# First attention block: scores as two fp32r matmuls over 128 partitions instead of one fp32 matmul over 64

## The chip, the cores and the metric

The kernel runs on one core of a Trainium2 chip. The core has five engines with a program each: TensorE (PE, with its weight loads shown apart as PEld), VectorE (DVE), ScalarE (ACT), GpSimd (POOL) and SyncE (SP), which here only issues DMAs. Each engine works through its own list in order and waits for others by semaphores. The metric is the time of one execution in microseconds (us) on the device; several runs are made and their median is given.

## The reference

Two transformer blocks over 512 tokens of width 1024, all in float32. What the change touches is the attention of the first block: 16 query heads of 64 dimensions share 2 key/value heads (8 query heads each), every token sees the 128 tokens up to itself, and each head has a sink logit in its softmax.

```
q, k, v, pz, ga, gp = jnp.split(xn @ w_in[l] + b_in[l], SPLITS, axis=-1)
sc = einsum('bhgqd,bkhd->bhgqk', q_block, k_two_blocks) / sqrt(64)   # 128 queries x 256 keys
sc = where(0 <= qpos - kpos < 128, sc, -1e30)
p  = softmax(concat([sc, sink]))[..., :-1]
y_a = (p @ v_two_blocks) @ w_attn_up
y_p = multiscale_pool(pz) @ w_pool_up
h = h + (sigmoid(ga) * y_a + sigmoid(gp) * y_p) @ w_o
```

Behind it stand, untouched, a mixture-of-experts layer (16 experts out of 16384 for each of 8 heads of a token) and a second block with dilated attention and a gated feed-forward.

## The kernel before, in words

Activations of the projections lie feature-major: 128 features on the partitions, 512 tokens in the free dimension. Each float32 matrix that is multiplied at full width is split into two fp32r parts, high (`whi`, `xh`) and low (`wlo`, `xl`), and a product is made of three fp32r matmuls (high-high, high-low, low-high: `mm3`, L137 to L140). One block of the input projection, 128 output features by 512 tokens, is 8 x 3 = 24 such matmuls (`zblock`, L234). The weights of a block come by a DMA on SP's queue into one of three raw buffers (`wload`, L127), ACT rounds them to the high part (L132) and DVE subtracts to get the low part (L134).

The input projection has 30 blocks: blocks 0 to 7 queries, 8 keys, 9 values, 10 to 13 the pooling branch, 14 to 29 the gates of the two branches. A query block holds two heads: head b of the first key/value group on partitions 0 to 63 and head b of the second on 64 to 127. DVE writes the queries with bias and the factor 1/8 to `qT` (L261); ACT writes keys and values with their bias (L263). `b_in`, `qT`, `kT` stay in SBUF.

Attention (L301 to L358) goes over 4 blocks of 128 queries (i) and 2 key/value groups (g). For each of 8 heads one fp32 matmul over the 64 partitions of the group makes 128 queries x 256 keys (128 keys for i = 0) of scores (L313); in the trace it shows as two records of the engine and two weight loads. Two heads share a PSUM tile `sc`, of which there are two. DVE adds the mask and takes the row maximum (L315), ACT takes the exponentials with their sum (L328), PE transposes the 128x128 pieces (L339), ACT and DVE by turns copy the transposes to SBUF (L342, L344), and PE multiplies them with the values (L348, fp32, two records each). DVE divides by the sums (L351), and the result is transposed and split for the next projection (L356).

The 16 gate blocks (L361 to L367) follow in the text, but no wait ties them to attention: the scheduler lays out each engine's list ahead of time by its own estimate of when things are ready, and puts matmuls of the gate blocks (`mm` in the rows) between those of attention. Their sigmoid is ACT's (L366). ACT holds one set of function tables at a time: between a sigmoid and an exponential it loads a table. The gates' results `sg` lie in the pool `sgp`, which stands until the block's end. After attention come `w_attn_up`, `w_pool_up`, the merge and `w_o`, and `hres`, the input for the residual, is loaded into the space that attention leaves (L370 to L372).

`gain` (L68) loads a row of 1024 gains into one of two buffers of the tag "gain": first g_mix, then g_ffn and ln_final_g, for the stages behind.

Of the kernel before, what the change touches and what calls it, by code (L numbers as in the profile page):

```python
# [8 lines left out]
F32 = mybir.dt.float32  # L9
F32R = mybir.dt.float32r  # L10
# [3 lines left out]
AF = mybir.ActivationFunctionType  # L14
OP = mybir.AluOpType
# [3 lines left out]
S = 512  # L19
# [24 lines left out]
def body(ctx: ExitStack, tc: tile.TileContext, A: dict, out: bass.AP):  # L44
    nc = tc.nc
    V, SC, PE, GP, SY = nc.vector, nc.scalar, nc.tensor, nc.gpsimd, nc.sync
# [19 lines left out]
    gn = ctx.enter_context(tc.tile_pool(name="gn", bufs=2, reuse_waits="tile"))  # L66
# [6 lines left out]
    def f(ap):  # L73
        return ap.bitcast(F32)
# [120 lines left out]
    with ExitStack() as st:  # L195
# [3 lines left out]
        sgp = st.enter_context(tc.tile_pool(name="sgp", bufs=1, reuse_waits="tile"))  # L199
# [42 lines left out]
        with ExitStack() as s1:  # L242
            psc = s1.enter_context(tc.tile_pool(name="psc", bufs=1, space=PSUM, reuse_waits="tile"))
            zp = s1.enter_context(tc.tile_pool(name="zp", bufs=1, reuse_waits="tile"))
# [4 lines left out]
            recip = zp.tile([128, 4, 16], F32, name="recip")  # L249
            SY.dma_start(recip, A["pool_recip"])  # L250

            qT = zp.tile([128, 8, S], F32, name="qT")
            kT = zp.tile([128, S], F32, name="kT")
            vT = zp.tile([128, S], F32, name="vT")
            vtok = zp.tile([128, NT, 128], F32, name="vtok")
# [1 line left out]
            for blk in [8, 9] + list(range(8)):  # L257
                ps = zblock(blk)
                b = b_in[:, blk:blk + 1]
                if blk < 8:  # L260
                    V.tensor_scalar(qT[:, blk, :], ps, b, 0.125, op0=OP.add, op1=OP.mult)  # L261
                else:
                    SC.activation(kT if blk == 8 else vT, ps, AF.Identity, bias=b)  # L263
            tps = pst.tile([128, 4, 128], F32, name="tr", tag="tr")
            for i in range(NT):
                PE.transpose(tps[:, i, :], vT[:, i * 128:(i + 1) * 128], ident)
# [2 lines left out]
            with ExitStack() as s2:  # L269
# [6 lines left out]
                for j in range(4):  # L276
                    ps = zblock(10 + j)
# [16 lines left out]
                    ps = psc.tile([128, S], F32, name="sc", tag="sc", bufs=2)  # L294
# [6 lines left out]
            for i in range(NT):  # L301
                nk = 1 if i == 0 else 2
                k0 = (i + 1 - nk) * 128
                o = att.tile([128, D], F32, name="otok", bufs=1)
                for g in range(2):
                    sl = slice(64 * g, 64 * g + 64)
                    mx = sm.tile([128, 8], F32, name="mx")
                    sb = att.tile([128, 8, 256], F32, name="sb")
                    for h in range(8):
                        if h % 2 == 0:  # L310
                            sp2 = psc.tile([128, 2, 256], F32, name="sc", tag="sc", bufs=2)
                        sp = sp2[:, h % 2]
                        PE.matmul(sp[:, :nk * 128], lhsT=qT[sl, h, i * 128:(i + 1) * 128],  # L313
                                  rhs=kT[sl, k0:k0 + nk * 128])
                        V.tensor_tensor_reduce(out=sb[:, h, :nk * 128], in0=sp[:, :nk * 128],  # L315
                                               in1=mask[:, 256 - nk * 128:], scale=1.0, scalar=-3.0e38,
                                               op0=OP.add, op1=OP.max, accum_out=mx[:, h:h + 1])
                    sk = sink[:, 8 * g:8 * g + 8]
                    m = sm.tile([128, 8], F32, name="m")
                    V.tensor_tensor(m, mx, sk, op=OP.max)  # L320
                    es = sm.tile([128, 8], F32, name="es")
                    V.tensor_tensor(es, sk, m, op=OP.subtract)
                    SC.activation(es, es, AF.Exp)
                    nm = sm.tile([128, 8], F32, name="nm")
                    V.tensor_scalar(nm, m, -1.0, None, op0=OP.mult)
                    sums = sm.tile([128, 8], F32, name="sums")
                    for h in range(8):
                        SC.activation(sb[:, h, :nk * 128], sb[:, h, :nk * 128], AF.Exp,  # L328
                                      bias=nm[:, h:h + 1], accum_out=sums[:, h:h + 1])
                    V.tensor_tensor(sums, sums, es, op=OP.add)  # L330
                    V.reciprocal(sums, sums)
                    po = psc.tile([128, 8, 64], F32, name="pv", tag="pv")
                    for hp in range(4):
                        tp = pst.tile([128, 4, 128], F32, name="tr", tag="tr")
                        pt = att.tile([128, 4, 128], F32, name="pt")
                        n = 0
                        for h in (2 * hp, 2 * hp + 1):
                            for k in range(nk):
                                PE.transpose(tp[:, n, :], sb[:, h, k * 128:(k + 1) * 128], ident)  # L339
                                n += 1  # L340
                        if hp % 2:
                            SC.activation(pt[:, :n, :], tp[:, :n, :], AF.Copy)  # L342
                        else:
                            V.tensor_copy(pt[:, :n, :], tp[:, :n, :])  # L344
                        n = 0
                        for h in (2 * hp, 2 * hp + 1):
                            for k in range(nk):
                                PE.matmul(po[:, h, :], lhsT=pt[:, n, :], rhs=vtok[:, i + 1 - nk + k, sl],  # L348
                                          start=(k == 0), stop=(k == nk - 1))
                                n += 1  # L350
                    V.tensor_tensor(o[:, g * 512:(g + 1) * 512].rearrange("p (h d) -> p h d", h=8), po,  # L351
                                    sums[:, :, None].to_broadcast([128, 8, 64]), op=OP.mult)
                for c in range(2):
                    tp = pst.tile([128, 4, 128], F32, name="tr", tag="tr")
                    for k in range(4):
                        PE.transpose(tp[:, k, :], o[:, (4 * c + k) * 128:(4 * c + k + 1) * 128], ident)  # L356
                    split_psum(tp, oh[:, 4 * c:4 * c + 4, i * 128:(i + 1) * 128],
                               ol[:, 4 * c:4 * c + 4, i * 128:(i + 1) * 128])  # L358

            gates = []  # L360
            for c in range(8):  # L361
                for w in range(2):
                    blk = 14 + 8 * w + c
                    ps = zblock(blk)
                    s_ = sgp.tile([128, S], F32, name=f"sg{w}{c}")
                    SC.activation(s_, ps, AF.Sigmoid, bias=b_in[:, blk:blk + 1])  # L366
                    gates.append(s_)  # L367

        resid = ctx.enter_context(tc.tile_pool(name="resid", bufs=1, side="right", reuse_waits="tile"))
        hres = resid.tile([128, NT, D], F32, name="hres")  # L370
# [2 lines left out]

        with ExitStack() as s1:
            pmx = s1.enter_context(tc.tile_pool(name="pmx", bufs=2, space=PSUM, reuse_waits="tile"))
            mh = ft.tile([128, ND, S], F32R, name="mh", tag="fh")
            ml = ft.tile([128, ND, S], F32R, name="ml", tag="fl")
            for c in range(8):
                sg = gates[2 * c:2 * c + 2]
                wh, wl = wload(A["w_attn_up"][c], [128, ND, 128])  # L380
                ps = pmm.tile([128, S], F32, name="mm", tag="mm")
                fm_block(ps, wh, wl, oh, ol, ND)
                V.tensor_tensor(sg[0], sg[0], ps, op=OP.mult)
                wh, wl = wload(A["w_pool_up"][c], [128, 4, 128])
                ps = pmm.tile([128, S], F32, name="mm", tag="mm")
                fm_block(ps, wh, wl, poh, pol, 4)
                V.tensor_tensor(sg[1], sg[1], ps, op=OP.mult)
                V.tensor_tensor(sg[0], sg[0], sg[1], op=OP.add)
                split_psum(sg[0], mh[:, c, :], ml[:, c, :])

            def to_h(c, t, ps):
                sl = slice(c * 512, (c + 1) * 512)
                V.tensor_tensor(hres[:, t, sl], hres[:, t, sl], ps, op=OP.add)

            sqrt_ahead(sg[0][:, 0:1])
            token_major([pmm] * 3 + [pmx], "w_o", range(2), ND, whole(mh), whole(ml), to_h)
# [3 lines left out]
    with ExitStack() as st:  # L400
# [87 lines left out]
        with mix as s1:  # L488
# [18 lines left out]
            for hp_ in range(16):  # L507
                if hp_ < len(first):
                    ps = first[hp_]
                else:  # L510
                    wh, wl = wload(A["w_query"][hp_], [128, ND, 128])
                    ps = pmm.tile([128, S], F32, name="mm", tag="mm")
# [5 lines left out]
                ps = psc.tile([128, NT, 128], F32, name="sc", tag="sc")  # L518
# [11 lines left out]
                h = hp_ // 2  # L530
# [176 lines left out]
        with tc.manual_schedule():  # L707
# [30 lines left out]
            for t in range(3):  # L738
                sl = slice(t * 128, (t + 1) * 128)
# [12 lines left out]
    with ExitStack() as st:  # L752
# [9 lines left out]
        with ExitStack() as s2:  # L762
# [23 lines left out]
            kk = tk.tile([128, NT, 8], F32, name="kk")  # L786
# [193 lines left out]
        with ExitStack() as s2:  # L980
# [12 lines left out]
            for c in range(22):  # L993
                if c < 2:
                    sg = sg01[:, c, :]
                else:
                    ps = fblock("w_gate", c)
                    sg = wk.tile([128, S], F32, name="sg")
                    SC.activation(sg, ps, AF.Silu)
                    ps = fblock("w_up", c)  # L1000
# [99 lines left out]
```

## Time and profile before

| | us |
|---|---|
| median of 3 runs | 2302.21 (2301.6 to 2306.77) |
| the profiled execution, its own time | 2305.47 |
| its span, first to last instruction | 2303.8 |
| PE busy | 2243.0 (97%) |
| DVE busy | 1493.0 (65%) |
| ACT busy | 978.6 (42%) |

The mean granted TensorE clock is 0.99 of full speed. A matmul's record is longer than the time it takes from the next one, since matmuls overlap in the engine: the pitch, from the start of one record to the start of the next, is what a matmul costs in a row of them. So PE reads as fully busy even where its pitch is longer than it need be, and the pitches have to be read from the timeline.

The attention of the first block lies between 108 and 208 us from the start of the span.

### The profile page before, as it was taken

Reading aid. Unit: us, or ns where it says so; the run is one execution under the profiler, and the core shown is the slowest. Engines: PE = TensorE matmul, PEld = TensorE weight load, DVE = VectorE, ACT = ScalarE, POOL = GpSimd, SP = SyncE. Lnnn points to the kernel's source line nnn. Section 1 sums busy time; section 2 is a strip of 40 time slices with the busy share of each in tenths; the row PEclk is TensorE's granted clock in tenths of the full one; section 3 lists DMA queues with packets and bytes.
Section 4 is the critical chain, followed back from the end, with each engine's and each line's share of the span. In section 5 each row is a group of like instructions: output and inputs, shape, how many; then the busy total and the mean of one; then the engine's idle time right before and its main releaser. Section 6 shows DMA issues by size and latency. Waiting matters only on the chain.

```text
span 2303.8 us, 30176 instructions
## 1 busy us (share of the span) xinstructions
PE 2243.0 (97%) x11337; PEld 1926.8 (84%) x11337; DVE 1493.0 (65%) x2998; ACT 978.6 (42%) x1629; POOL 358.1 (16%) x261
## 2 busy tenths in 40 slices
PE   7999998999899999999999999999999999999998
PEld 6768887989799999888888888888866778888886
DVE  4553254999999994777778777777774656333323
ACT  4354233333897783333333333333353364232221
POOL 0000000000222431333333333333300000000000
PEclk9999999999899999999999999999999999999999
DMA  5202232443678998998889888998732112333331
GB/s 174 91 19 75 90 109 88 128 124 116 210 271 292 364 347 275 322 320 302 308 322 325 301 308 286 315 329 310 268 99 71 55 55 93 103 98 99 93 101 65
DMA packets 177571, 444.82 MB, mean 193 GB/s; under 512 B 15248, under 2 KB 84240, under 8 KB 174352
## 3 DMA queue, kind: packets, MB, share of 16 engines
q1 hardware_dynamic: 140560, 308.65, 40.1%
q0 software_dynamic: 36864, 134.23, 16.6%
q8 instruction: 89, 1.46, 0.3%
q14 instruction: 58, 0.48, 0.1%
HBM read 402.19 MB, written 40.63 MB: 192 GB/s over the span
## 4 chain that ended last, share of the span: by engine, by line
PE 84%; DVE 6%; ACT 4%; issue 3%; DMA 2%; POOL 0%; SPq 0%; DVEq 0%; ACTq 0%; POOLq 0%
PE mm L138 13%; PE mm L139 13%; PE mm L140 12%; PE acc L140 7%; PE acc L138 7%; PE acc L139 6%; PE hps L140 6%; PE hps L138 6%; PE hps L139 6%; PE wps L614 2%; PE sc L313 1%; ACT stg L616 1%; PE pv L348 1%; PE sc L892 1%; DVE wlo L134 1%
## 5 line engine op out<-in xcount | busy, mean ns | idle before, releaser
L132 ACT ACTIVATE whi<-wraw 128x1024 fp32r<-128x1024 f32 x232 | 242.1, 1046 | 567.5 <-PE mm L139 342.6
L134 DVE TENSOR_TENSOR wlo<-wraw,whi 128x1024 fp32r<-128x1024 f32 x232 | 279.3, 1206 | 267.8 <-ACT whi L132 263.3
L138 PE MATMUL hps<-x2h,whi 128*128 128x384 f32 x1024 | 347.9, 340 | 2.0 <-ACT whi L132 1.8
L140 PE MATMUL hps<-x2h,wlo 128*128 128x384 f32 x1024 | 345.1, 337 | 1.4 <-DVE wlo L134 0.8
L139 PE MATMUL hps<-x2l,whi 128*128 128x384 f32 x1024 | 344.1, 336 | 0.0
L466 POOL DMA_INDIRECT gu<-in_u_experts_dram,ix x128 | 178.2, 1392 | 918.1 <-DVE og L608 608.8
L138 PE MATMUL acc<-whi,hh 128*128 128x512 f32 x768 | 302.0, 393 | 10.9 <-ACT hh L119 10.9
L140 PE MATMUL acc<-whi,hl 128*128 128x512 f32 x768 | 303.2, 395 | 1.3 <-DVE hl L120 1.3
L139 PE MATMUL acc<-wlo,hh 128*128 128x512 f32 x768 | 301.5, 393 | 0.0
L666 DVE TENSOR_TENSOR wlo<-wraw,whi 128x1024 fp32r<-128x1024 f32 x188 | 228.2, 1223 | 84.6 <-ACT whi L664 82.6
L664 ACT ACTIVATE whi<-wraw 128x1024 fp32r<-128x1024 f32 x188 | 196.3, 1053 | 117.2 <-issue 49.1
L475 POOL DMA_INDIRECT gv<-in_v_experts_dram,ix x128 | 178.6, 1395 | 382.0 <-DVE hres L477 266.5
L138 PEld LDWEIGHTS hps<-x2h,whi 128*128 128x128 f32 x1024 | 193.3, 189 | 5.6 <-ACT whi L132 2.1
L139 PEld LDWEIGHTS hps<-x2l,whi 128*128 128x128 f32 x1024 | 193.0, 189 | 2.7
L140 PEld LDWEIGHTS hps<-x2h,wlo 128*128 128x128 f32 x1024 | 193.0, 189 | 2.1 <-DVE wlo L134 1.1
L138 PEld LDWEIGHTS acc<-whi,hh 128*128 128x128 f32 x768 | 145.3, 189 | 44.3 <-ACT hh L119 16.2
L140 PEld LDWEIGHTS acc<-whi,hl 128*128 128x128 f32 x768 | 145.0, 189 | 35.7 <-DVE hl L120 5.7
L119 ACT ACTIVATE hh<-hw 128x384 fp32r<-128x384 f32 x128 | 67.3, 526 | 249.4 <-DVE hw L687 249.4
L139 PEld LDWEIGHTS acc<-wlo,hh 128*128 128x128 f32 x768 | 145.3, 189 | 28.9
L477 DVE SCALAR_TENSOR_TENSOR hres<-gv,ga,hres 128x1024 f32<-128x1024 f32 x128 | 164.2, 1283 | 3.5 <-DMA gv<-in_v_experts_dram,ix 2.3
L468 DVE CUSTOM_DVE_ANT_0 gu<-gu,xtok 128x1024 f32<-128x1024 f32 x128 | 154.2, 1222 | 0.0
L139 PE MATMUL mm<-x4l,whi 128*128 128x512 f32 (+1 forms) x384 | 143.0, 373 | 0.0
(315 smaller groups left out, 4099.2 us busy)
## 6 DMA issues: line engine op xcount, KB each, us to landing
wraw<-in_u_cols_dram SPq DMA_DIRECT2D x128, 512.0 KB
wraw<-in_v_experts_dram SPq DMA_DIRECT2D x128, 512.0 KB
wraw<-in_w_in_dram SPq DMA_DIRECT2D x50, 512.0 KB
wdr<-stg SPq DMA_DIRECT2D x24, 1024.0 KB
wt<-wdr SPq DMA_DIRECT2D x16, 1536.0 KB
park<-hg SPq DMA_DIRECT2D x68, 192.0 KB
hg<-park SPq DMA_DIRECT2D x68, 192.0 KB
wraw<-in_w_gate_dram SPq DMA_DIRECT2D x22, 512.0 KB
```

What stands on the lines that cost most here:

```text
L119: SC.activation(hi, ps, AF.Copy)
L132: SC.activation(hi, raw, AF.Copy)
L134: V.tensor_tensor(lo, raw, f(hi), op=OP.subtract)
L138: PE.matmul(ps, lhsT=ah, rhs=bh, start=start, stop=False)
L139: PE.matmul(ps, lhsT=ah, rhs=bl, start=False, stop=False)
L140: PE.matmul(ps, lhsT=al, rhs=bh, start=False, stop=stop)
L466: GP.indirect_dma_start(out=u, out_offset=None, in_=A["u_experts"], in_offset=bass.IndirectOffsetOnAxis(ap=ix[:, s_:s_ + 1], axis=0))
L468: V.tensor_tensor_reduce(out=u, in0=u, in1=xtok, scale=1.0, scalar=0.0, op0=OP.mult, op1=OP.add, accum_out=a[:, s_:s_ + 1])
L475: GP.indirect_dma_start(out=v, out_offset=None, in_=A["v_experts"], in_offset=bass.IndirectOffsetOnAxis(ap=ix[:, s_:s_ + 1], axis=0))
L477: V.scalar_tensor_tensor(hres[:, 0, :], v, a[:, s_:s_ + 1], hres[:, 0, :], op0=OP.mult, op1=OP.add)
L664: SC.activation(hi, raw, AF.Copy)
L666: V.tensor_tensor(lo, raw, f(hi), op=OP.subtract)
```

## The change

The query blocks are kept twice, as `qs[0]` and `qs[1]`, one for each key/value group, each over all 128 partitions. In `qs[g]` the group's own 64 partitions hold the fp32r high part of the query (ACT) and the other 64 partitions the low part, query minus high (DVE). The keys of group g, with the factor 1/8, are split too: `kk[:, g]` holds the high part on both halves of the partitions, `kl[:, g]` the low part on both. One fp32r matmul of `qs[g]` with `kk` sums, over its 128 partitions, (high + low) x key high, a second one adds (high + low) x key low. `kk` and `kl` take the two buffers of "gain". Since the queries now take twice the space, `sgp` holds only the gates of c = 0 to 3; the gates of c = 4 to 7 go to a new pool `sgq` that is opened after attention's pools are closed.

```diff
-            qT = zp.tile([128, 8, S], F32, name="qT")
+            qs = [zp.tile([128, 8, S], F32R, name=f"qs{g}") for g in range(2)]
+            kk = gn.tile([128, 2, S], F32R, name="kk", tag="gain")
+            kl = gn.tile([128, 2, S], F32R, name="kl", tag="gain")
+            own = (slice(0, 64), slice(64, 128))
...
-                if blk < 8:
-                    V.tensor_scalar(qT[:, blk, :], ps, b, 0.125, op0=OP.add, op1=OP.mult)
-                else:
+                if blk >= 8:
                     SC.activation(kT if blk == 8 else vT, ps, AF.Identity, bias=b)
+                for g in range(2):
+                    me, other = own[g], own[1 - g]
+                    if blk < 8:
+                        q = qs[g][me, blk, :]
+                        SC.activation(q, ps[me], AF.Identity, bias=b[me])
+                        V.scalar_tensor_tensor(qs[g][other, blk, :], ps[me], b[me], f(q), op0=OP.add, op1=OP.subtract)
+                    elif blk == 8:
+                        for rows in (me, other):
+                            SC.activation(kk[rows, g, :], kT[me], AF.Copy, scale=0.125)
+                            V.scalar_tensor_tensor(kl[rows, g, :], kT[me], 0.125, f(kk[me, g, :]),
+                                                   op0=OP.mult, op1=OP.subtract)
...
-                        PE.matmul(sp[:, :nk * 128], lhsT=qT[sl, h, i * 128:(i + 1) * 128],
-                                  rhs=kT[sl, k0:k0 + nk * 128])
+                        ks = slice(k0, k0 + nk * 128)
+                        qi = qs[g][:, h, i * 128:(i + 1) * 128]
+                        PE.matmul(sp[:, :nk * 128], lhsT=qi, rhs=kk[:, g, ks], start=True, stop=False)
+                        PE.matmul(sp[:, :nk * 128], lhsT=qi, rhs=kl[:, g, ks], start=False, stop=True)
...
-            for c in range(8):
+            def gate(pool, c):
                 for w in range(2):
...
+            for c in range(4):
+                gate(sgp, c)
...
+            sgq = s1.enter_context(tc.tile_pool(name="sgq", bufs=1, reuse_waits="tile"))
+            for c in range(4, 8):
+                gate(sgq, c)
```

The change also moves instructions, since the scheduler lays out the lists anew. On PE, in the second of the four query blocks, the kernel before has this, where `sc` are scores, `tr` transposes, `pv` products with the values and `mm` matmuls of the gate blocks:

```order
L348 MATMUL pv<-vtok,pt 128x64 x4
L339 MATMUL tr<-ident,sb 128x128 x4
L313 MATMUL sc<-kT,qT 128x256
L140 MATMUL mm<-xh,wlo 128x512
L348 MATMUL pv<-vtok,pt 128x64 x8
```

The changed kernel's PE in the third query block, with `qs_326` and `qs_327` for the two groups:

```order
L328 MATMUL sc<-kk,qs_326 128x256
L329 MATMUL sc<-kl,qs_326 128x256
L139 MATMUL mm<-xl,whi 128x512
L140 MATMUL mm<-xh,wlo 128x512
L138 MATMUL mm<-xh,whi 128x512
L328 MATMUL sc<-kk,qs_327 128x256
L329 MATMUL sc<-kl,qs_327 128x256
L139 MATMUL mm<-xl,whi 128x512
L363 MATMUL pv<-vtok,pt 128x64 x8
```

Each score is two rows now, one with the high and one with the low part of the keys. Between the first score and the last transpose of attention stood 80 matmuls of the gate blocks; now 125 stand there, 89 of them ahead of or just behind the last score.

On ACT, in the middle of attention, the changed kernel has more sigmoids (`sg`) between the exponentials (`sb`), each with a table load in front and one behind:

```order
L343 ACTIVATE sb,sums<-sb,nm 128x256 x8
L357 ACTIVATE pt<-tr 128x512
L382 ACT_TABLE_LOAD
L382 ACTIVATE sg_1733<-mm,b_in 128x512
L357 ACTIVATE pt<-tr 128x512
L338 ACT_TABLE_LOAD
L338 ACTIVATE es<-es 128x8
```

From the first sigmoid to the last copy of attention's output there were 4 sigmoids and 5 table loads; there are 6 and 11.

On SP, the weights of the gates (`in_w_in`), the gains and the residual input `hres`:

```order
-L130 DMA wraw<-in_w_in_dram 128x1024 x17
-L372 DMA hres<-in_x_dram 128x1024
+L130 DMA wraw<-in_w_in_dram 128x1024 x18
+L70 DMA gain<-in_g_ffn_dram 128x1024
+L70 DMA gain<-in_ln_final_g_dram 128x1024
 L130 DMA wraw<-in_w_in_dram 128x1024
```

The two gains wait until the last score has been made, since `kk` and `kl` hold their buffers; the loads of the last six gate blocks stand behind them, and five of these behind `hres`, which waits for attention's space as before. From the gate blocks' end on, all five lists are the same as before.

## Rows read from the trace of the kernel before

**Rows 1.** The page: the chain that ended last, by engine.

```profile
PE 84%; DVE 6%; ACT 4%; issue 3%; DMA 2%; POOL 0%; SPq 0%; DVEq 0%; ACTq 0%; POOLq 0%
```

**Rows 2.** Stretches: length, busy us (instructions) of PE, PEld, DVE, ACT, POOL; clock, DMA.

```profile
34.00:76.00 42.00, 42.00 (x187) 34.74 (x186) 14.85 (x15) 7.88 (x9) 0.00 (x0) 1.00 0.36 110
108.24:196.05 87.81, 87.81 (x495) 61.74 (x495) 47.48 (x194) 47.35 (x149) 0.00 (x0) 1.00 0.06 19
196.05:208.11 12.06, 12.06 (x87) 10.64 (x85) 5.05 (x11) 8.63 (x23) 0.00 (x0) 1.00 0.06 8
```

**Rows 3.** PE by line, 108.24 to 196.05 us: records, busy us, mean ns.

```profile
L313 PE MATMUL sc<-kT,qT 64*128 64x256 f32 x96 | 29.9, 419 | 0.0
L348 PE MATMUL pv<-vtok,pt 128*128 128x64 f32 x184 | 24.0, 277 | 0.0
L339 PE MATMUL tr<-ident,sb 128*128 128x128 f32 x96 | 16.2, 281 | 0.0
L139 PE MATMUL mm<-xl,whi 128*128 128x512 f32 x20 | 8.8, 441 | 0.0
...
L313 PE MATMUL sc<-kT,qT 64*128 64x128 f32 x32 | 5.8, 310 | 0.0
L356 PE MATMUL tr<-ident,otok 128*128 128x128 f32 x24 | 3.7, 275 | 0.0
```

**Rows 4.** PE timeline in attention, 137.8 us on: start us, length us, records.

```profile
137.83 1.13 PE L313 MATMUL sc<-kT,qT 64*128 64x256 f32 x4
138.89 0.50 PE L139 MATMUL mm<-xl,whi 128*128 128x512 f32 x1
139.32 0.70 PE L313 MATMUL sc<-kT,qT 64*128 64x256 f32 x2
139.95 0.44 PE L339 MATMUL tr<-ident,sb 128*128 128x128 f32 x2
140.31 0.70 PE L313 MATMUL sc<-kT,qT 64*128 64x256 f32 x2
```

**Rows 5.** PE timeline at 29.5 us: fp32r matmuls of 256 columns.

```profile
29.49 0.28 PE L138 MATMUL mm<-xh,whi 128*128 128x256 f32 x1
29.61 0.28 PE L139 MATMUL mm<-xl,whi 128*128 128x256 f32 x1
```

**Rows 6.** PE timeline at 403.6 us: fp32 matmuls over 128 partitions between fp32r ones.

```profile
403.49 0.28 PE L140 MATMUL mm<-x2h,wlo 128*128 128x256 f32 x1
403.61 1.05 PE L520 MATMUL sc<-sk,q 128*128 128x128 f32 x8
404.42 0.42 PE L138 MATMUL hps<-x2h,whi 128*128 128x384 f32 x1
404.68 0.34 PE L139 MATMUL hps<-x2l,whi 128*128 128x384 f32 x1
```

**Rows 7.** PE timeline at 114 us: pairs of scores of the first query block.

```profile
114.23 0.71 PE L313 MATMUL sc<-kT,qT 64*128 64x128 f32 x4
114.87 0.50 PE L140 MATMUL mm<-xh,wlo 128*128 128x512 f32 x1
115.21 0.40 PE L138 MATMUL mm<-xh,whi 128*128 128x512 f32 x1
115.53 0.49 PE L313 MATMUL sc<-kT,qT 64*128 64x128 f32 x4
115.96 0.50 PE L139 MATMUL mm<-xl,whi 128*128 128x512 f32 x1
```

**Rows 8.** Waits of PE's weight loads, 108.5 to 208 us: total us, times, longest.

```profile
PEld sc L313 <- DVE mx L315: 4.1, 13, 0.4
```

**Rows 9.** ACT by line, 108.24 to 208.11 us: busy, mean ns, idle before, releaser.

```profile
L342 ACT ACTIVATE pt<-tr 128x512 f32<-128x512 f32 x12 | 7.1, 595 | 20.4 <-PE tr L339 20.3
...
L366 ACT ACT_TABLE_LOAD x3 | 3.8, 1283 | 0.1
```

**Rows 10.** DVE by line, 34 to 80 us.

```profile
L261 DVE TENSOR_SCALAR qT<-mm,b_in 128x512 f32<-128x512 f32 x8 | 6.0, 751 | 26.5 <-PE mm L140 26.5
```

More of the change, by code (lines that the diff above doesn't have):

```diff
@@ L364, in body @@
                     ps = zblock(blk)
-                    s_ = sgp.tile([128, S], F32, name=f"sg{w}{c}")
+                    s_ = pool.tile([128, S], F32, name=f"sg{w}{c}")
                     SC.activation(s_, ps, AF.Sigmoid, bias=b_in[:, blk:blk + 1])
                     gates.append(s_)
+            for c in range(4):
+                gate(sgp, c)
         resid = ctx.enter_context(tc.tile_pool(name="resid", bufs=1, side="right", reuse_waits="tile"))
```

## The prediction

> **What bounds the kernel now.** I read the chain of waits first: 84% of it is TensorE [rows 1], so time is won where TensorE works longer than it must. Next the stretches: the first block's attention runs from 108.24 us (its first score) to 208.11 us (its last transpose). TensorE is busy there without a gap, DVE for 52.5 of 99.9 us, ACT for 56.0; the granted clock is 1.00, that is 2.4 GHz [rows 2]. A busy TensorE need not be a fast one, so the third view is its timeline, for the pitch from one start to the next, and the fourth its instructions by line, for the counts.
>
> Pitches. A score of 128x256 (two records) that stands alone takes 0.63 us (139.32 to 139.95, 140.31 on the same pattern); two in a row take 1.06 us (137.83 to 138.89), so the second adds 0.43, 0.215 a record, and the first carries 0.20 us more [rows 4]. A score of 128x128 has half the columns: 0.107 a record. A full fp32r matmul of 512 columns: 187 instructions in 42.00 us, 0.225; I take 0.226 [rows 2]. fp32 records over 128 partitions: 8 in 0.81 us with the next one following at once, 0.101, and 0.853 us if the matmul behind them is charged its usual 0.17; I take 0.108 for transposes and value products [rows 6].
>
> Counts by those pitches, from 108.24 to 196.05 us, where all the scores lie [rows 3]: 60 gate matmuls (L139's 20, and as many of L138 and L140) and 3 of the pooling branch x 0.226 = 14.2 us; 96 + 24 transposes and 184 value records x 0.108 = 32.8; 96 score records x 0.213 and 32 x 0.107 = 23.9. Together 70.9 us, and the stretch is 87.81 us long: 16.9 us are in no pitch. The check is the stretch behind, 196.05 to 208.11 us, with 23 gate matmuls and 64 transposes and value records but no score: 5.2 + 6.9 = 12.1 us by the same pitches, in 12.06. So the 16.9 us belong to the scores. They stand in 47 places on the timeline, 0.36 us for each: 0.20 in the score itself, the rest in its neighbours (the gate matmul at 138.89 takes 0.43 instead of 0.226, two transposes at 139.95 take 0.36 instead of 0.22) [rows 4].
>
> What is special about them? Not fp32: at 403.61 us eight fp32 records over all 128 partitions stand between fp32r matmuls, and the whole passage from 403.61 to 404.68 is 1.07 us against 0.85 + 0.17, 0.05 us too long instead of 0.36 [rows 6]. The scores are the only instructions here on 64 partitions (64*128 in the rows). This is the point on which the sum rests.
>
> The Trainium skill, TensorEngine Tiling (Array Packing), section Key Properties, says that changing the tiling mode drains TensorE. The trace agrees with a cost at each change, 0.36 us for going in and out. By that rule the whole 16.9 us go with the change; without it only the difference of the pitches would.
>
> **The change, part by part.**
>
> The scores. Removed: 23.9 us of score records. Added: 128 fp32r matmuls. Those of 256 columns have a pitch of 0.12 us [rows 5]: 96 x 0.12 = 11.5. For 32 of 128 columns over 128 partitions the trace has no fp32r row; the nearest are 0.108 for an fp32 record of 128 columns and 0.213 for a whole fp32 product of 128 columns, so 3.5 to 6.8 us; I take 0.12, as the 256-column ones, 3.8. Sum 15.3, gain 8.6 us (5.6 to 8.9).
>
> The 47 places. All matmuls now lie over 128 partitions, so I take the 16.9 us as gone. Bounds: 0 (the cost stays with the scores for a reason I don't see) and 16.9.
>
> Speaking against the change: a half of the array that is given up. In the first query block a pair with both scores in one group takes 0.64 us (114.23 to 114.87), a pair of different groups 0.43 (115.53 to 115.96) [rows 7]: the two halves ran at once. The Trainium skill, TensorE: Matmul & The Clock Gate, Part 3 (packing small matmuls), has the same: matmuls on different row groups run concurrently. If all heads were paired so, 64 scores would cost half of 23.9, 12 us, and two full-array matmuls for each would be the dearer form. But only 4 pairs on the timeline are (2 of 128 and 2 of 256 columns), about 1.3 us, and that is already inside the 87.81 us; the sum isn't changed.
>
> Waits. TensorE's weight loads for scores waited 13 times for DVE's row maximum, 4.1 us in all [rows 8]; part of this lies inside the 16.9. With faster scores TensorE comes to DVE sooner, and 52 instead of 47 places have scores by the order of the instructions. I charge 3 us; bounds 0 and 8 (twice what is named).
>
> ACT. Two more sigmoids, two more weight roundings and six more table loads of 1.28 us [rows 9] fall into attention, since 125 gate matmuls instead of 80 stand there: 7.7 us for the tables, about 11 us in all. So ACT has 56.0 + 11 = 67 us of work in a stretch that is to last 99.9 - 22 + 45 x 0.226 = 88 us. Behind each sigmoid on ACT's list wait the exponentials of the next group and, behind these, TensorE's transposes. The cover is the gate matmuls between: ACT's copies waited 20.4 us for TensorE's transposes before [rows 9], so ACT was early, and 11 us fit into that. I charge nothing beyond the 3 us; the price without cover is a rival below.
>
> The splits of queries and keys. For each of 8 blocks, instead of one DVE operation of 0.75 us [rows 10], two on ACT and two on DVE. The length is 512 columns as before, so I take 0.75 for each, 64 partitions or not: 1.5 us on ACT and 0.75 more on DVE, and 3 us instead of 0.75 until the PSUM buffer is free. From 34 to 76 us ACT is busy for 7.9 and DVE for 14.9 of 42.0 us, while TensorE runs at its pitch without a hole [rows 2]; a block takes 24 x 0.226 = 5.4 us and there are three buffers. DVE idles 26.5 us there waiting for TensorE [rows 10]. Cost nothing; without cover 8 x 2.25 = 18 us, which would need a TensorE that waits for a buffer, and none of the three is asked for within 3 us. The eight splits of the keys (6 us) have until 108 us.
>
> The gates of c = 4 to 7, SP's list. The gains wait for the last score, and the loads of the last six gate blocks behind them. At the last score TensorE has 36 gate matmuls of attention's stretch still ahead (125 less 89), and at attention's end the rest of the seventh block and three whole ones, 84 x 0.226 = 19 us, before the first of the six is needed. No cost; the bound is a load and its split, under 10 us, if attention ended that late.
>
> Sum: -8.6 - 16.9 + 3 = -22.5 us, within attention; from 208 us on the lists are the same and start earlier. I take 22. The profiled execution took 2305.47 us, 1.7 of it outside its span of 2303.8; it would take 2283.5. It lies 3.3 us above the median of the runs, 2302.21; a median after of 2280 follows.
>
> **The rivals.**
>
> The cost of the 47 places isn't that of 64 partitions and stays, for instance because it comes with each first matmul into a fresh PSUM tile. For it: part of the waits at scores are named as DVE's. Against: the quiet passage in rows 6. Then -8.6 + 3 = -5.6 and, with the same 0.36 us at five more places, about -4: 2298.
>
> ACT takes part of the gain: six table loads that land between exponentials and transposes, 7.7 us, and one rounding of 1 us each before two sigmoids. Then -22.5 + 10 = -12.5: 2290. For it: 67 us of work in 88, and an in-order list. Against: the 20.4 us of slack.
>
> Slower. ACT becomes the bound: its idle time of 99.9 - 56.0 = 43.9 us doesn't shrink, since each sigmoid waits for the last of its block's 24 matmuls, with exponentials queued behind it, and two more sigmoids hold the list for up to a block, 5.4 us each. Attention then lasts 67 + 43.9 + 10.8 = 122 us, less the 45 gate matmuls done inside it, 10.2: 12 us more than before, 2314. It decides once ACT idles for more than 43 us in the stretch (99.9 + 10.2 - 67). Against: nearly all of that idle time is waiting for TensorE, which gets faster.
>
> The change doesn't do what it says: fp32r over 128 partitions runs no faster than 0.213 for 256 columns. Rows 5 speak against it; then 27.3 us replace 23.9 and the 16.9 still go, -10: 2292. I give this no chance of its own.
>
> **How the numbers follow.** Chances: forecast 0.70, with a range of its own from 2274 (no wait charged, the small matmuls cheap, and 2 us of runs' scatter) to 2286 (waits 8 us); ACT takes part 0.14; the 47 places stay 0.11; slower 0.05. A change of less than 0.3%, 6.9 us, can't be told from none here. Faster by more: the first two, 0.84; within 0.3%: the third and a fifth of the fourth, 0.12; slower: the rest of the fourth, 0.04. The range for 8 in 10: 2273 to 2292, which takes in ACT's part and leaves out the last two cases.
>
> **What would show it.** Attention from first score to last transpose at 84 to 90 us with some 45 more gate matmuls inside; a pair of score matmuls at 0.24 us wherever it stands; the gate matmul next to a score at 0.226 to 0.24, not 0.33 to 0.43. The forecast is wrong if single scores still carry 0.2 us, if weight loads wait for ACT's exponentials for more than a few us, or if TensorE has holes between 34 and 76 us or after attention's end.

## The result and the profile after

The changed kernel takes 2279.96 us (median of 5 runs, 2278.24 to 2283.24), the kernel before in the same session 2304.44 us (2301.6 to 2306.77). The ratio is 0.9897, 95% interval 0.9886 to 0.9908: 24.5 us less. The forecast was 2280 us and 22 us less. The profiled execution took 2283.24 us with a span of 2281.5 us, 22.3 us under the span before.

The chain of waits, by engine, is TensorE's as before [rows 1]:

```profile
PE 84%; DVE 6%; ACT 5%; issue 4%; DMA 2%; POOL 0%; SPq 0%; DVEq 0%; ACTq 0%; POOLq 0%
```

The stretches answer to [rows 2] (length; busy us and instructions of PE, PEld, DVE, ACT, POOL; granted clock; DMA share; GB/s). Attention now runs from 108.95 us to its last four transposes, which start at 197.23 us and end at 197.58, where the next instruction starts:

```profile
34.00:76.00 42.00, 42.00 (x187) 34.77 (x186) 22.25 (x26) 19.76 (x25) 0.00 (x0) 1.00 0.36 107
108.95:197.90 88.95, 88.83 (x627) 77.70 (x626) 53.25 (x207) 67.24 (x183) 0.00 (x0) 1.00 0.14 45
```

From 34 to 76 us the splits have added 11.9 us to ACT and 7.4 to DVE, and TensorE did its 187 instructions in 42.00 us all the same. To the end of those transposes attention lasts 88.6 us instead of 99.9 (both are counted from a matmul of the pooling branch, 0.3 to 0.4 us ahead of the first score), with 125 gate matmuls inside instead of 80. The 45 more are work taken from behind it, 45 x 0.226 = 10.2 us, so attention gained 11.3 + 10.2 = 21.5 us; it starts 0.7 us later, which leaves 20.8. The first addition to the residual behind it, on DVE's timeline of the kernel before and then of the changed one (start us, length us):

```profile
349.20 0.69 DVE L393 TENSOR_TENSOR hres<-hres,mm 128x512 f32<-128x512 f32 x1 [0.40 <-PE mm L140]
```

```profile
328.46 0.69 DVE L415 TENSOR_TENSOR hres<-hres,mm 128x512 f32<-128x512 f32 x1 [0.40 <-PE mm L140]
```

It comes 20.7 us earlier, and the rest, 1.6 us up to the end of the span, lies in the later stages. Their instructions are the same, so I put it down to scatter; that is not shown.

How a score runs now, on TensorE's timeline (start us, length us, records), to be held against [rows 4]:

```profile
136.47 0.82 PE L354 MATMUL tr<-ident,sb 128*128 128x128 f32 x6
137.05 0.37 PE L328 MATMUL sc<-kk,qs 128*128 128x256 f32 x1
137.25 0.28 PE L329 MATMUL sc<-kl,qs 128*128 128x256 f32 x1
137.37 0.28 PE L328 MATMUL sc<-kk,qs 128*128 128x256 f32 x1
137.49 0.28 PE L329 MATMUL sc<-kl,qs 128*128 128x256 f32 x1
137.60 0.40 PE L138 MATMUL mm<-xh,whi 128*128 128x512 f32 x1
137.83 0.40 PE L139 MATMUL mm<-xl,whi 128*128 128x512 f32 x1
138.07 0.38 PE L328 MATMUL sc<-kk,qs 128*128 128x256 f32 x1
138.28 0.28 PE L329 MATMUL sc<-kl,qs 128*128 128x256 f32 x1
138.40 1.89 PE L363 MATMUL pv<-vtok,pt 128*128 128x64 f32 x16
```

Two scores take 0.55 us (137.05 to 137.60) where they took 1.06, one takes 0.33 (138.07 to 138.40) where it took 0.63, and the gate matmul behind them 0.23, where it took 0.43. Inside, the pitch is 0.11 to 0.12; here the first matmul of a place takes 0.20 to 0.21. Between gate matmuls it can run at its plain pitch too, and a whole score then takes 0.23 (130.15 to 130.38):

```profile
130.15 0.28 PE L328 MATMUL sc<-kk,qs 128*128 128x256 f32 x1
130.26 0.28 PE L329 MATMUL sc<-kl,qs 128*128 128x256 f32 x1
130.38 0.40 PE L139 MATMUL mm<-xl,whi 128*128 128x512 f32 x1
```

The weight loads' waits in that stretch (us in total, times, longest), answering to [rows 8]:

```profile
PEld sc L328 <- DVE mx L330: 2.9, 13, 0.3
PEld pv L363 <- ACT pt L357: 1.5, 4, 0.5
PEld pv L363 <- DVE pt L359: 1.0, 4, 0.3
```

### The profile page after: what moved, and what is told of

Same layout as the page of the kernel before. It is cut to its first block, busy times and chain, and to the rows that moved or that the text cites. A ratio compares the mean times of both kernels' runs of the same rounds, so it can differ in the third digit from the quotient of the medians.

```text
span 2281.5 us, 30213 instructions
## 1 busy us (share of the span) xinstructions
PE 2222.8 (97%) x11337; PEld 1924.1 (84%) x11337; DVE 1500.5 (66%) x3010; ACT 999.0 (44%) x1655; POOL 357.4 (16%) x261
## 4 chain that ended last, share of the span: by engine, by line
PE 84%; DVE 6%; ACT 5%; issue 4%; DMA 2%; POOL 0%; SPq 0%; DVEq 0%; ACTq 0%; POOLq 0%
PE mm L138 13%; PE mm L139 13%; PE mm L140 13%; PE acc L138 7%; PE acc L140 7%; PE acc L139 7%; PE hps L140 6%; PE hps L138 6%; PE hps L139 6%; PE wps L636 2%; ACT stg L638 1%; PE pv L363 1%; PE sc L914 1%; PE pv L940 1%; DVE wlo L134 1%
```

## The experiments

All were timed in 5 rounds beside the kernel before, which took 2304.29 us in the first session (the first three below and the last one) and 2303.06 us in the second. The changed kernel's 2279.96 us belong to the session of the result, with 2304.44 us before, so a difference from it is good to a microsecond or two only. "Stage" is attention, from its first instruction on TensorE to the start of its last four transposes.

**fp32 over 128 partitions.** The one fp32 matmul a score stays; only the other 64 partitions are filled, with zeros.

```diff
-            qT = zp.tile([128, 8, S], F32, name="qT")
+            qs = [zp.tile([128, 8, S], F32, name=f"qs{g}") for g in range(2)]
+            for g in range(2):
+                GP.memset(qs[g][own[1 - g]], 0.0)
...
+                        V.tensor_scalar(qs[g][own[g], blk, :], ps[own[g]], b[own[g]], 0.125, op0=OP.add, op1=OP.mult)
...
+                        qi = qs[g][:, h, i * 128:(i + 1) * 128]
+                        PE.matmul(sp[:, :nk * 128], lhsT=qi, rhs=kT[:, ks])
```

> Scores stay fp32, one matmul a head with two records, but over all 128 partitions: the query block of each group has zeros on the other group's 64 partitions. PE's list is that of the kernel before (47 places with scores, 80 gate matmuls in attention). If the 0.36 us a place comes with the 64 partitions, 47 x 0.36 = 16.9 us go, less up to 3 us of waits: 2288 to 2291 us, and a lone score of 128x256 takes 0.43 us instead of 0.63. If the cost comes with fp32, with a fresh PSUM tile or with the waits for DVE, nothing goes: 2304 +- 2 us.

Measured: 2289.16 us (2287.65 to 2294.29), ratio 0.9930 [0.9915, 0.9944], 15.1 us less than before. The array does no more useful work, no instruction is cheaper by itself, and three fifths of the gain are there. TensorE's timeline of this run:

```profile
135.05 0.38 PE L345 MATMUL tr<-ident,sb 128*128 128x128 f32 x2
135.27 0.60 PE L320 MATMUL sc<-kT,qs 128*128 128x256 f32 x2
135.71 0.60 PE L345 MATMUL tr<-ident,sb 128*128 128x128 f32 x4
136.14 0.60 PE L320 MATMUL sc<-kT,qs 128*128 128x256 f32 x2
```

A lone score takes 0.44 us (135.27 to 135.71) instead of 0.63, its two records' pitch and no more, and the four transposes behind it 0.43, their own 0.108 each. So the cost at the 47 places is that of 64 partitions among 128, 0.32 us a place by the medians. It isn't that of a fresh PSUM tile, the prediction's other reading, since the PSUM tiles and TensorE's order are those of the kernel before. The rest of the gain, 2289.16 - 2279.96 = 9.2 us, is the step from one fp32 to two fp32r matmuls, with the new order that goes with it.

**fp32r, own 64 partitions only.** The changed kernel with both score matmuls on the group's own half; the query's low part is left out of the product.

```diff
-                        qi = qs[g][:, h, i * 128:(i + 1) * 128]
-                        PE.matmul(sp[:, :nk * 128], lhsT=qi, rhs=kk[:, g, ks], start=True, stop=False)
-                        PE.matmul(sp[:, :nk * 128], lhsT=qi, rhs=kl[:, g, ks], start=False, stop=True)
+                        qi = qs[g][sl, h, i * 128:(i + 1) * 128]
+                        PE.matmul(sp[:, :nk * 128], lhsT=qi, rhs=kk[sl, g, ks], start=True, stop=False)
+                        PE.matmul(sp[:, :nk * 128], lhsT=qi, rhs=kl[sl, g, ks], start=False, stop=True)
```

> The changed kernel, with its two fp32r matmuls a score over only the group's own 64 partitions (the query's low part is left out of the scores). PE's list is that of the changed kernel, 52 places. If the drain comes with 64 partitions, 52 x 0.36 = 18.7 us come back, less what the changed kernel waits there already (3.7 us): 2295 to 2299 us, and a score's two matmuls take about 0.44 instead of 0.24 to 0.32 us. If the drain was one of fp32, or of single scores, it stays at 2280 us.

Measured: 2309.24 us (2301.59 to 2314.94), ratio 1.0016 [1.0005, 1.0027], 29 us more than the changed kernel with the same order of instructions. That is above what was expected. On the timeline the stop at a score is back:

```profile
164.26 0.28 PE L328 MATMUL sc<-kk,qs 64*128 64x256 f32 x1
164.38 0.28 PE L329 MATMUL sc<-kl,qs 64*128 64x256 f32 x1
164.59 0.50 PE L140 MATMUL mm<-xh,wlo 128*128 128x512 f32 x1
164.93 0.40 PE L138 MATMUL mm<-xh,whi 128*128 128x512 f32 x1
```

Inside the 64 partitions the pitch is the same 0.12; the last score matmul before the change back takes 0.21 and the gate matmul behind it 0.34 instead of 0.23. The other part of the excess was not foreseen. The stretches of this run show the granted clock (the third figure from the end):

```profile
108.00:116.00 8.00, 8.00 (x37) 5.34 (x35) 4.36 (x18) 5.03 (x6) 0.00 (x0) 1.00 0.24 68
116.00:124.00 8.00, 8.00 (x28) 5.00 (x28) 3.29 (x25) 3.71 (x18) 0.00 (x0) 0.65 0.00 0
124.00:148.00 24.00, 24.00 (x83) 18.19 (x82) 7.74 (x31) 8.20 (x25) 0.00 (x0) 0.50 0.00 1
148.00:156.00 8.00, 8.00 (x33) 5.02 (x32) 4.39 (x15) 5.82 (x19) 0.00 (x0) 0.93 0.23 66
156.00:200.00 44.00, 44.00 (x286) 34.90 (x285) 23.17 (x93) 28.58 (x76) 0.00 (x0) 1.00 0.08 25
```

The clock falls to 1.2 GHz from about 118 to 149 us and comes back while the same kind of work goes on. If all of TensorE's work there takes twice as long, that cost 8 x 0.35 + 24 x 0.50 + 8 x 0.07 = 15.4 us, an estimate. The stage lasted 116.0 us against 88.3 in the changed kernel, first instruction to last transpose's start; so 27.7 - 15.4 = 12.3 us are left for 52 places, 0.24 us each. (The profiled execution took 2314.94 us, the longest of this run's.)

**Gates only.** The kernel before with its gates in two pools as in the change.

```diff
+            def gate(pool, c):
...
-            for c in range(8):
+            for c in range(4):
+                gate(sgp, c)
...
+            sgq = s1.enter_context(tc.tile_pool(name="sgq", bufs=1, reuse_waits="tile"))
+            for c in range(4, 8):
+                gate(sgq, c)
```

> The kernel before, with the gates of c = 4 to 7 moved to a pool behind attention as in the change, scores untouched. PE's list in attention is as before (47 places, 80 gate matmuls). Theory: 2304 +- 2 us, the move is worth nothing by itself. Rival (the gain comes from where the gates lie): 2294 us or less.

Measured: 2302.76 us (2299.44 to 2305.55), ratio 0.9990 [0.9979, 1.0002]: no difference. The later gates cost nothing and bring nothing.

**One score matmul.** The changed kernel without the matmul of the key's low part.

```diff
-                        PE.matmul(sp[:, :nk * 128], lhsT=qi, rhs=kk[:, g, ks], start=True, stop=False)
-                        PE.matmul(sp[:, :nk * 128], lhsT=qi, rhs=kl[:, g, ks], start=False, stop=True)
+                        PE.matmul(sp[:, :nk * 128], lhsT=qi, rhs=kk[:, g, ks], start=True, stop=True)
```

> Changed kernel with one score matmul a head instead of two: the product with the key's low part is left out, the other keeps 128 partitions, and the order of the rest stays. Theory (TensorE bounds the stage, and a score matmul costs its pitch): 48 matmuls of 256 columns at 0.12 us and 16 of 128 at 0.11 go away, which is 7.5 us less: 2271 to 2275 us against 2280. Rival (VectorE's maxima or ScalarE end last once TensorE has less to do): the waits of the score matmuls for VectorE's mx grow by what is saved, 2278 to 2280.

Measured: 2272.16 us (2271.73 to 2274.51), ratio 0.9868 [0.9853, 0.9883]: 7.8 us less than the changed kernel by the medians, 6.4 if each is held against the kernel before of its own session, where 7.5 were worked out from the pitches. Contrary to what was expected the scheduler changed the order too: 141 gate matmuls stand in the stage instead of 125. The scores' waits for DVE fell rather than grew:

```profile
PEld sc L328 <- DVE mx L329: 1.9, 8, 0.5
```

So in the changed kernel, too, DVE and ACT don't set the pace of the stage: what a score matmul's pitch saves on TensorE comes off the time, to within that uncertainty.

**Gates without table loads.** The changed kernel with exp in place of the gates' sigmoid.

```diff
-                    SC.activation(s_, ps, AF.Sigmoid, bias=b_in[:, blk:blk + 1])
+                    SC.activation(s_, ps, AF.Exp, bias=b_in[:, blk:blk + 1])
```

> Changed kernel with the gates' sigmoid replaced by exp, the function that the softmax of the same stage uses, so that ScalarE loads no other table between them (the gates' values are others). Theory (ScalarE's work in this stage, loads of tables among it, lies beside TensorE's): no difference beyond 2 us, 2278 to 2282 us. Rival (ScalarE takes part of the gain): six loads of 1.28 us less on ScalarE give back most of 7.7 us, 2272 to 2275 us.

Measured: 2282.36 us (2280.94 to 2288.74), ratio 0.9917 [0.9903, 0.9931], against 0.9897 [0.9886, 0.9908]: no gain; the median is 2.4 us higher and lies 0.4 us above the expected range, and the overlapping intervals don't say whether that is anything. The scheduler laid out another order here, with 104 gate matmuls in the stage instead of 125, so this is not the removal of the table loads alone; but with each gate matmul taken off at 0.226 us, attention to the end of its last transposes takes 62.1 us here and 60.4 in the changed kernel, no gain either. ACT's lines of the changed kernel in attention (busy us, mean ns):

```profile
L382 ACT ACT_TABLE_LOAD x6 | 7.7, 1283 | 0.1
L338 ACT ACT_TABLE_LOAD x5 | 6.4, 1283 | 0.1
```

and of this run, from 105 to 200 us, all that is left:

```profile
L382 ACT ACT_TABLE_LOAD x1 | 1.3, 1283 | 0.0
```

Some 12.8 us of ACT's table loads are gone and the time didn't fall: ACT's part was hidden, as forecast. The rival by which ACT took most of 10 us falls.

**Both halves in turn.** The kernel before with the heads of its two groups alternating, so that neighbouring scores use different halves; fp32, 64 partitions each.

```diff
-                    for h in range(8):
-                        if h % 2 == 0:
-                            sp2 = psc.tile([128, 2, 256], F32, name="sc", tag="sc", bufs=2)
+                for h in range(8):
+                    if h % 2 == 0:
+                        sps = [psc.tile([128, 2, 256], F32, name="sc", tag="sc", bufs=2) for _ in range(2)]
+                    for g in range(2):
+                        sl = slice(64 * g, 64 * g + 64)
+                        PE.matmul(sps[g][:, h % 2, :nk * 128], lhsT=qT[sl, h, i * 128:(i + 1) * 128],
+                                  rhs=kT[sl, k0:k0 + nk * 128])
```

> Kernel before with the heads of its two groups in turn: fp32 scores on 64 partitions each, of the lower and the upper half one after the other, so that two neighbours use different halves. No place is saved but by the new order (40 places and not 47). Theory (what was gained is the switch between 64 and 128 partitions, a cost per place): 7 places at 0.36 us, 2.5 us less than 2304, and up to 4 us more where two scores of different halves run 0.43 us as a pair and not 0.64 (the rows at 114 us of the kernel before); 2296 to 2303 us. Rival (the gain came from scores that use the whole array, however it is filled): 12 us or more less, 2292 or below. Either is worse by some us if the two groups' PSUM tiles wait for VectorE's mx.

Measured: 2297.99 us (2294.95 to 2301.01), ratio 0.9977 [0.9968, 0.9986]: 5.1 us less than before, within the first theory's range. TensorE's timeline shows both facts at once:

```profile
143.10 0.86 PE L312 MATMUL sc<-kT,qT 64*128 64x256 f32 x4
143.88 0.51 PE L139 MATMUL mm<-xl,whi 128*128 128x512 f32 x1
144.32 0.70 PE L312 MATMUL sc<-kT,qT 64*128 64x256 f32 x2
144.95 0.50 PE L140 MATMUL mm<-xh,wlo 128*128 128x512 f32 x1
145.28 0.39 PE L138 MATMUL mm<-xh,whi 128*128 128x512 f32 x1
```

Two scores of different halves take 0.78 us (143.10 to 143.88) and not 1.06, so the halves do overlap; but each place still ends in a gate matmul of 0.44 or 0.33 instead of 0.23, and single scores still take 0.63. Filling the array in this way, with 40 places instead of 47, is worth a fifth of the change; by the count of the expectation about half of that fifth is the fewer places.

**Low key part on 64 partitions.** The changed kernel with the second score matmul alone on the own half, to part the stop from the clock.

```diff
-                        PE.matmul(sp[:, :nk * 128], lhsT=qi, rhs=kl[:, g, ks], start=False, stop=True)
+                        PE.matmul(sp[:, :nk * 128], lhsT=qs[g][sl, h, i * 128:(i + 1) * 128], rhs=kl[sl, g, ks], start=False, stop=True)
```

> Changed kernel with the second score matmul on the own 64 partitions alone (query's high part with the key's low part; low with low is left out), the first still on 128; same order and count. Theory (the cost of a place is the switch of the partitions, not a rate of 64-partition matmuls, and the clock falls only where all score matmuls use 64): one switch there and one back at each of 52 places, 0.2 us each as the run with both halves showed at full clock, 10 us more than 2280: 2288 to 2292 us, granted clock above 0.95 in the stage. Rival (any 64-partition fp32r matmul lowers the clock): clock below 0.9 in 110 to 200 us, 2298 to 2312 us. Second rival (a second switch within each score counts too): more than 0.3 us a place, 2296 us or above at full clock.

Measured: 2307.91 us (2303.42 to 2318.24), ratio 1.0022 [1.0010, 1.0034]. My theory fell, and the time lies where both rivals had it. The clock fell again, earlier and for a shorter time:

```profile
108.00:116.00 8.00, 8.00 (x34) 5.60 (x33) 4.41 (x19) 3.96 (x5) 0.00 (x0) 1.00 0.22 68
116.00:132.00 16.00, 16.00 (x50) 12.00 (x51) 5.42 (x31) 6.29 (x31) 0.00 (x0) 0.50 0.00 0
132.00:140.00 8.00, 8.00 (x48) 6.30 (x46) 3.42 (x15) 5.40 (x12) 0.00 (x0) 0.93 0.00 0
140.00:220.00 80.00, 79.93 (x484) 64.01 (x483) 39.16 (x141) 51.38 (x136) 0.00 (x0) 1.00 0.13 40
```

and at full clock each change of the partitions shows by itself on TensorE's timeline, at 128 columns and at 256:

```profile
112.39 0.33 PE L328 MATMUL sc<-kk,qs 128*128 128x128 f32 x1
112.64 0.33 PE L329 MATMUL sc<-kl,qs 64*128 64x128 f32 x1
112.90 0.50 PE L139 MATMUL mm<-xl,whi 128*128 128x512 f32 x1
...
150.83 0.36 PE L328 MATMUL sc<-kk,qs 128*128 128x256 f32 x1
151.12 0.38 PE L329 MATMUL sc<-kl,qs 64*128 64x256 f32 x1
151.43 0.38 PE L328 MATMUL sc<-kk,qs 128*128 128x256 f32 x1
151.75 0.38 PE L329 MATMUL sc<-kl,qs 64*128 64x256 f32 x1
152.06 0.50 PE L138 MATMUL mm<-xh,whi 128*128 128x512 f32 x1
```

The three behind the first of the four take 0.31 to 0.32 us where the changed kernel has 0.11 to 0.12 inside a place: 0.2 us for a change, from 128 to 64 and from 64 to 128. At 128 columns (112.39 to 112.90 us) they take 0.25 to 0.26 instead of 0.11, 0.14 to 0.15 for a change. The first of a place, 0.29 behind a transpose, has 0.20 in the changed kernel as well, so 0.09 of it is the change. The stage lasts 113.9 us, 25.6 more than the changed kernel's 88.3; 16 x 0.5 + 8 x 0.07 = 8.6 us of it are the clock, by the same estimate, and 17 us are left for 64 scores, 0.27 each, or 0.33 for each of the 52 places.

**The same for the second block.** The changed kernel, with the second block's fp32 scores also laid over 128 partitions, the other head's half filled with zeros (one more copy a token tile, on ACT).

```diff
-            qk_T = [tk.tile([128, 4, S], F32, name=f"qkT{w}", tag=f"qkT{w}") for w in range(2)]
+            qz = [tk.tile([128, 4, S], F32, name=f"qz{p}", tag="qkT0" if p == 0 else "qz1") for p in range(2)]
+            for p in range(2):
+                GP.memset(qz[p][hv[1 - p]], 0.0)
...
+                        V.tensor_copy(qz[0][hv[0], :, ts_], tp[hv[0]])
+                        SC.activation(qz[1][hv[1], :, ts_], tp[hv[1]], AF.Copy)
...
-                    PE.matmul(sp[:, :N], lhsT=qk_T[0][sl, h // 2, t * 128:(t + 1) * 128], rhs=qk_T[1][sl, h // 2, :N])
+                    PE.matmul(sp[:, :N], lhsT=qz[h % 2][:, h // 2, t * 128:(t + 1) * 128], rhs=kT2[:, h // 2, :N])
```

> The changed kernel, and in the second block the scores go over 128 partitions too, still in fp32: queries of even and odd heads in two tiles with zeros on the other 64 partitions. The second block's scores stand in 32 places of the trace before, each 0.20 us too long and with about 0.22 us more in the neighbours, 0.42 x 32 = 13.4 us. Theory: 8 to 13 us less than the changed kernel, 2267 to 2272 us. Rival (that stretch waits for DVE's row maxima, 23 us by the trace, and hides the drains): 2277 to 2280 us.

Measured: 2274.13 us (2270.56 to 2274.69), ratio 0.9858 [0.9841, 0.9876]; that is 5.8 us under the changed kernel by the medians, 8.5 by the spans of the profiled executions (2273.0 and 2281.5). That is a miss of 2 us against the range expected, between the theory and its rival. One period of a score and seven matmuls of a projection, first the changed kernel, then this run:

```profile
1735.73 1.12 PE L914 MATMUL sc<-qkT,qkT 64*128 64x512 f32 x2
...
1738.62 1.12 PE L914 MATMUL sc<-qkT,qkT 64*128 64x512 f32 x2
```

```profile
1735.06 1.12 PE L922 MATMUL sc<-kT,qz 128*128 128x512 f32 x2
...
1737.66 1.02 PE L922 MATMUL sc<-kT,qz 128*128 128x512 f32 x2
```

2.89 us became 2.60, 0.29 less. From the first to the last of these 32 places the stretch shortened from 101.7 to 93.0 us in the two traces, 8.7 us or 0.27 a place. The gain per place is smaller than the 0.42 I had read there; the traces show the 8 us that were expected at the least, the medians less. Of the versions that keep every term of the scores this is the fastest, and it beats both kernels.

## Why the prediction was right

Its sum was -8.6 for the pitches, -16.9 for the places, +3 for waits. The two main causes are the ones that the runs show; the places are worth about 2 us less than forecast, the pitches with the waits about 1 us more. With each gate matmul taken off at 0.226 us, attention to the end of its last transposes takes 81.8 us in the trace before, 67.3 in the one with zeros and 60.4 in the one with the change: 14.5 and 6.9 less, 21.4 together, against the 22.5 of the sum. The medians differ by 24.5; the other 3 us lie behind attention or in the scatter of the runs, and no run here tells which. That the median fell on 2280 to a tenth is luck: the forecast took 22 us from a median of 2302.21, and the kernel before took 2304.44 beside the changed one.

The places. Forecast -16.9, 0.36 us a place; measured -15.1 by the medians of the run with zeros and -14.5 by its trace, 0.31 to 0.32 a place. The prediction's one point of doubt, whether this cost belongs to the 64 partitions, is settled by three runs: filled with zeros the stop goes; fp32r on 64 partitions brings it back; both halves in turn leave it. By the rule of the Trainium skill that the prediction drew on, TensorEngine Tiling (Array Packing), Key Properties, the engine drains at a change of mode. These runs agree that there is a cost at each change. Its size with fp32r is 0.14 to 0.2 us by the run with the low key part on 64 partitions. The 47 places became 52 by the new order, and no stop shows at them on the timeline.

The reading behind the 16.9 has small slips. The check on the stretch without scores counts 23 gate matmuls, but two of these only touch its ends; 21 start in it, which makes 11.7 us in 12.06, so that 0.4 us in 12 are in no pitch where no score stands, and not all of the 16.9 need be the scores'. In the same way 59, not 60, start in the stretch with the scores. And the 0.853 us for eight fp32 records doesn't come out of [rows 6]: 1.07 less 0.17 is 0.90, or 0.113 a record, against the 0.108 that was taken. Also, 108.24 us is the start of a pooling matmul; the first score starts at 108.67.

The pitches. Forecast -8.6; at the pitches of the changed kernel, 0.117 for 96 matmuls and 0.11 for 32, it is 9.1. The step from zeros to the change measured -9.2 by the medians and -6.9 by the traces; waits and the new order are in both. The 32 matmuls of 128 columns, for which I had no row, have a pitch of 0.11 (I took 0.12): a choice between 0.108 and 0.213 that came out well.

The waits. Forecast +3 (0 to 8); named in the trace are 2.9 us for DVE and 2.5 for ACT's and DVE's copies before the value products, some of it under other matmuls; 9.1 by pitch against 6.9 in the traces leaves about 2. What the forecast had not quite right is the form: "0.24 us wherever it stands" holds for 0.23 to 0.26 between gate matmuls, but many scores take 0.32 to 0.34, because the first matmul of the place takes 0.20 or more. The trace shows two reasons for these 0.08 us. Behind transposes it is no cost: the last record ahead of the score is as much shorter, so that the six transposes at 136.47 and the score matmul behind them take 0.78 us, 6 x 0.108 + 0.12 = 0.77. (Behind value products, at five places, that record is shorter by 0.03 only.) Behind gate matmuls it is a wait for DVE: of 15 such places with 256 columns, the first matmul takes 0.12 to 0.14 at the seven where its weight load was early, as at 130.15, and 0.21 to 0.23 at the eight where DVE's row maximum held that load, as at 138.07.

ACT. Forecast 67 us of work in 88; measured 67.24 in 88.95, with 11 table loads, ten of which are gone in the run with exp without any gain: the slack seen in [rows 9] was there. The rivals "ACT takes part" and "ACT becomes the bound" fall on that run and on the time of the change.

The splits and the gates. TensorE's 187 instructions in 42.00 us and the run with the gates alone show both at nothing, as charged.

A way to be slower that the prediction doesn't name is the clock: with fp32r scores on 64 partitions, the same order of work ends above the kernel before. In the change as made, whose matmuls all fill 128 partitions, it stayed at 1.00 throughout attention.

## What to carry to other kernels

Matmuls over 64 partitions that stand singly among matmuls over 128 pay at each change, here 0.14 to 0.2 us per change with fp32r and 0.32 for going in and out with fp32; look for them on the timeline as a neighbour with a longer pitch (0.34 to 0.44 where 0.23 is usual), since no busy share shows them. A longer first matmul alone is no such sign: add the record in front of it before calling it a cost. The simplest cure tried here is zeros in the other half, worth 15.1 us; then that half can hold a second term, and the step to two fp32r matmuls was worth 7 to 9 more. In a stage that TensorE bounds, count by pitch and put what is in no pitch down to the places where it lies.

## What was not expected

The granted clock fell to 0.50 inside attention in both kernels with fp32r scores on 64 partitions (about 116 to 133 us in one, 118 to 149 in the other) and came back by itself. It stayed at 1.00 there with fp32 scores on 64 partitions (before, the gates alone, both halves in turn) and with fp32 or fp32r on 128. The fall isn't one of a single execution: the clock's mean over the whole span is 0.983 to 0.988 and 0.984 to 0.990 in all executions of these two, and 0.991 to 0.993 in those of the changed kernel. What TensorE did before the fall was the first query block, scores of 128 columns with a few gate matmuls between, and a stop at each change. Its records leave no hole there, before the fall or in it (8.00 us busy of 8.00 from 108 to 116 us), but the stops lie inside the records, so an engine that stands still for a moment can't be told from a busy one. The Trainium skill, TensorE: Matmul & The Clock Gate, Part 1, has the clock fall when TensorE is idle, for a stretch or, in one kernel, briefly and often. The records of these two runs show no idle stretch, and whether the stops are such brief idling is not shown. The changed kernel and the two differ in the partitions that the score matmuls use (and in what the low parts add), at the same order of instructions, so the 64 partitions belong to the cause; the kernels with fp32 on 64 have another order, so what fp32r adds to it stays open.
